# The weights' low parts written by ScalarE and an adding DMA instead of VectorE

## The chip, the cores and the metric

The kernel runs on one core of a Trainium2 chip. The metric is the device time of one execution in microseconds; the kernel before takes 945.7 us (median of three runs, 945.38 to 946.27).

## What is computed

One layer of a hybrid decoder trunk on 512 tokens of width 1024 in float32: a norm, three token mixers on one combined projection (windowed attention, a Conformer convolution of 31 taps, a gated short convolution), a gated merge, an output projection with residual, a gated MLP with a convolution of three taps, and a final norm. Cut to its core:

```python
u = rms_norm(x, norm1_g) @ w_in            # q k v | conf_a conf_gate | sc_b sc_c sc_x | gates
attn  = attention(q, k, v) @ w_attn_out
conf  = silu(layer_norm(dwconv31(conf_a * sigmoid(conf_gate)))) @ w_conf_out
short = (sc_b * dwconv3(sc_c * sc_x)) @ w_sc_out
x = x + (g0 * attn + g1 * conf + g2 * short) @ w_o
f_gate, f_val = split(dwconv3(rms_norm(x, norm2_g) @ w_up))
return rms_norm(x + (silu(f_gate) * f_val) @ w_down, final_g)
```

## The kernel before

**Weights.** All matrices are packed on the host in the order in which they are used: 1280 blocks of 128x128, eight to a chunk, so 160 chunks of 128x1024 float32 (512 KB each, `wts[c]`). TensorE takes each number as two parts, `hi` (the number cast to fp32r) and `lo` (the rest, cast too). A block is multiplied in three matmuls, hi·hi, hi·lo and lo·hi (`mm3`, L189 to L193; `down`, L845 to L847), so a chunk is 24 matmuls of 512 columns.

**The stream.** `prep(c)` (L150) loads chunk c from the SyncE queue into a float32 tile `w32` (L157; four buffers), and `w_split` makes the parts: ScalarE casts `w32` to `hi` (L170), VectorE subtracts, `lo = w32 - hi` (L171). `hi` and `lo` have `WB` = 4 buffers each. `take` (L177) hands out blocks and calls `prep` up to `AHEAD` = 2 chunks ahead of the one in use. A load thus waits until the subtraction has freed a `w32` buffer, and a cast until TensorE has done with the chunk that held the `hi` buffer. Chunks 0 and 1 are loaded in pieces at the start of the program, between the loads of x (L212 to L222), and split in quarters between the splits of x (L316).

**Who sets the order.** Each engine and each queue runs its instructions in a fixed order, in which a framework's scheduler has put them by readiness and by their place in the source; `tc.issue_after(q)` keeps what follows behind `q` on its engine. `anchor[0]` holds the last subtraction of a chunk's split, and the convolution's taps (a queue of VectorE tasks, `Queue.run`, L282) are put behind it. The zeros that `k_blocks` writes (L444) and the last norm's product (L874) are GpSimd's only other work.

**Other places that the rows name.** L237 and L238 split x for the first products (`xg`); L787, L790 and L812 evacuate and convolve a tile of the MLP's first product; L656 and L657 load two constants after the Conformer's products; the last three chunks (`KEEP` = 3, L890 to L896) are used a token tile at a time, then the final norm follows.

Of the kernel before, what the change touches and what calls it, by code (L numbers as in the profile page):

```python
# [10 lines left out]
F32 = mybir.dt.float32  # L11
# [28 lines left out]
GAP = 2  # L40
BUSY, FREE = 2.4, 2.7

# columns of the packed per-channel parameters
G1, G2 = 0, 8
CW = 16
CB = CW + KC * CONF_K
# [4 lines left out]
NPAR = FW + 2 * KF * 3  # L51


# the branches in the order of their merge: matrix, place of the gate, row blocks
BRANCHES = (("w_sc_out", 2, KC), ("w_attn_out", 0, 2), ("w_conf_out", 1, KC))


def weight_units():
    """The order in which 128x128 blocks of the weights are used: (matrix, row block, column block)."""
    aw = CONF // P  # L60
    a0, g0 = 18, 18 + aw
    b0, c0, x0 = 30, 36, 42
    gate0 = 48
    u = []
    for j in range(KC):
        for k in range(KD):
            u += [("w_in", k, a0 + j), ("w_in", k, g0 + j)]
    for g in range(3):
        for m in (0, 6):
            for p in range(2):  # L70
                u += [("w_in", k, m + 2 * g + p) for k in range(KD)]
        if g == 0:
            for k in range(KD):
                u += [("w_in", k, 12 + p) for p in range(2)]
    for k in range(KD):
        u += [("w_in", k, 14 + p) for p in range(4)]
    for j in range(KC):
        for m in (c0, x0, b0):
            u += [("w_in", k, m + j) for k in range(KD)]
    for name, br, n in BRANCHES:  # L80
        for s in range(KD + 1):
            if s < KD:
                u += [("w_in", k, gate0 + br * KD + s) for k in range(KD)]
            if s >= 1:
                u += [(name, k, s - 1) for k in range(n)]
    for j in range(KD):
        u += [("w_o", k, j) for k in range(KD)]
    for j in range(KF):
        for m in (j, KF + j):
            u += [("w_up", k, m) for k in range(KD)]  # L90
    for k in range(KF):
        u += [("w_down", k, c) for c in range(KD)]
    assert len(u) == N_UNITS
    return u


def score_bias():
    """ALiBi and the masks, by head pair: [4, 128, 512], from shapes alone."""
    slopes = np.exp2(-8.0 * np.arange(1, N_HEADS_ALL + 1, dtype=np.float32) / np.float32(N_HEADS_ALL)).astype(np.float32)
    i = np.arange(P)  # L100
    out = np.zeros((4, P, 512), np.float32)
    q, k = i[:, None], np.arange(256)[None, :]
    steps = q + P - k
    ok = (steps >= 0) & (steps <= 128)
    for p in range(2):
        for h in range(2):
            b = np.where(ok, -(slopes[2 * p + h] * steps.astype(np.float32)), np.float32(NEG))
            out[p, :, h * 256 : (h + 1) * 256] = b
    s1 = i[:, None] - i[None, :]
    s2 = s1 // 4  # L110
    ok1 = (s1 >= 0) & (s1 <= 128)
    ok2 = (s1 >= 0) & (s2 <= 128) & (s1 % 4 == 0)
    for p in range(2):
        for h in range(2):
            b1 = np.where(ok1, -(slopes[4 + 2 * p + h] * (s1 * 4).astype(np.float32)), np.float32(NEG))
            b2 = np.where(ok2, -(slopes[8 + 2 * p + h] * (s2 * 16).astype(np.float32)), np.float32(NEG))
            out[2 + p, :, h * 256 : h * 256 + 128] = b1
            out[2 + p, :, h * 256 + 128 : (h + 1) * 256] = b2
    return out
# [10 lines left out]
def trunk(ctx: ExitStack, tc: tile.TileContext, xT, wts, par, bias, sel, ident, fg, out):  # L130
# [13 lines left out]
    def ps512(name="ps"):  # L144
        return pp.tile([P, 512], F32, tag="ps", name=name)

    # ---- the stream of weights: loaded, and split into two parts that TensorE takes exactly
    chunks = {}

    def prep(c, load=((0, UNIT * P),), work=True):  # L150
        if c not in chunks:
            w32s[c] = wp.tile([P, UNIT * P], F32, tag="w32", name=f"w32_{c}", bufs=4)
            hi = wp.tile([P, UNIT * P], F32R, tag="whi", name=f"whi_{c}", bufs=WB)
            lo = wp.tile([P, UNIT * P], F32R, tag="wlo", name=f"wlo_{c}", bufs=WB)
            chunks[c] = (hi, lo)
        for a, b in load:
            nc.sync.dma_start(w32s[c][:, a:b], wts[c][:, a:b])  # L157
        if work:
            with ExitStack() as order:
                if c == 2:  # L160
                    for q in last:
                        order.enter_context(tc.issue_after(q))
                w_split(c, slice(0, UNIT * P))

    w32s = {}
    anchor = [None]

    def w_split(c, s):
        hi, lo = (q[:, s] for q in chunks[c])
        A.copy(hi, w32s[c][:, s])  # L170
        anchor[0] = V.tensor_tensor(out=lo, in0=w32s[c][:, s], in1=hi.bitcast(F32), op=ALU.subtract).ins  # L171

    WB = 4
    AHEAD = 2
    state = {"unit": 0, "prepped": 0}

    def take(n=1):  # L177
        """The next n blocks, as (hi, lo) of [128, n * 128]."""
        u = state["unit"]
        c, o = divmod(u, UNIT)  # L180
        assert o + n <= UNIT
        while state["prepped"] <= min(c + AHEAD, N_UNITS // UNIT - 1):
            prep(state["prepped"])
            state["prepped"] += 1
        state["unit"] += n
        hi, lo = chunks[c]
        return hi[:, o * P : (o + n) * P], lo[:, o * P : (o + n) * P]

    def mm3(ps, w, x, first, last):  # L189
        """ps += w.T @ x, each given as its two parts."""  # L190
        T.matmul(ps, w[0], x[0], start=first, stop=False)  # L191
        T.matmul(ps, w[0], x[1], start=False, stop=False)  # L192
        T.matmul(ps, w[1], x[0], start=False, stop=last)  # L193

    # ---- inputs and constants
    zero = cp.tile([P, WIDE], F32R, name="zero")
    V.memset(zero.bitcast(F32), 0.0)
    warm = ps512("warm")
# [29 lines left out]
    last = []  # L228

    def split(src, name, hi_scale=None, into=None):  # L230
        """Two parts of an SBUF or PSUM tile (times a per-partition factor)."""
        hi, lo = into or (t512(F32R, name + "h"), t512(F32R, name + "l"))
        if hi_scale is None:
            A.copy(hi, src)
# [15 lines left out]
        return split(acc, name + "s")  # L250

    def colsum(hi, lo, name):
        """Sums over all channels, on every partition: PSUM [128, 512]."""
        ps = ps512(name + "ps")
        T.matmul(ps, ones, hi, start=True, stop=False)
        T.matmul(ps, ones, lo, start=False, stop=True)
        return ps

    def rsqrt_of(ps, n, name):
        """(ps / n + eps) ** -0.5, with one Newton step."""  # L260
        a = t512(name=name + "a")
        V.tensor_scalar(out=a, in0=ps, scalar1=1.0 / n, scalar2=EPS, op0=ALU.mult, op1=ALU.add)
        y = t512(name=name + "y")
# [5 lines left out]
        V.scalar_tensor_tensor(out=r, in0=y, scalar=1.5, in1=r, op0=ALU.add, op1=ALU.mult)  # L269
        return r  # L270

    # ---- work that runs beside the matrix products, a little at a time
    class Queue:
        def __init__(self):
            self.q = deque()
# [14 lines left out]
        def drain(self):  # L290
            self.run(1e9)

    # ---- chains of work with TensorE in them: each link some slots after the one before it
    due = {}
    now = [0]
    starts = deque()
# [2 lines left out]
        due.setdefault(now[0] + n, []).append(fn)  # L299

    def slot():
        """Between two tiles of matrix products."""
        now[0] += 1
        for fn in due.pop(now[0], ()):
            fn()
        if starts and now[0] % EVERY == 0:
            starts.popleft()()
        conv.run(BUSY if due else FREE)

    # ---- first norm: the products start on x * g, and the rows' factors come in behind them  # L310
    xg = []
    for k in range(KD):
        with ExitStack() as order:
# [22 lines left out]

    hn = [None] * KD

    # ---- Conformer branch: gated input, 31 taps, layer norm, SiLU
    conv = Queue()  # L340
    apad = []
    cacc = [None] * KC
# [73 lines left out]

        conv.add(mean_sum, 5)

    # ---- attention
    def perm(ap):  # L420
        """Tokens by their residue modulo 4."""
        return ap.rearrange("p (i c) -> p c i", c=4)

    def qk_tile(name, permuted):
# [11 lines left out]
        return hi, lo  # L436

    def k_blocks(name):
        """The keys of two heads, by token tiles: the first head's rows beside the second's, zeros elsewhere."""
        hi, lo = (kp.tile([P, 1024], F32R, tag="kb", name=name + n) for n in "hl")  # L440
        v = lambda q, h: q[h * HD : (h + 1) * HD].rearrange("p (t h i) -> p t h i", t=4, h=2)
        for q in (hi, lo):
# [13 lines left out]
    stats = {}  # L456

    def v_tiles(s, n):
        """Values with the tokens on partitions: n columns for each of the four token tiles."""
        pss = [ps512(f"pv{s}{t}") for t in range(4)]  # L460
        for k in range(KD):
            wh, wl = take(n // P)
# [17 lines left out]
        slot()  # L480

    def block(s, t, p, qk, nm, l):
        """Two heads' scores, weights and weighted values for one tile of queries."""
        n = 128 if (s == 0 and t == 0) else 256
        sc = t512(name=f"sc{s}{t}{p}")
        scv = sc[:, : 2 * n].rearrange("p (h k) -> p h k", h=2)
# [115 lines left out]
            tt(U[0, p], U[0, p], U[1, p], ALU.add)  # L602
            oT[p] = split(U[0, p], f"oT{p}")

    # ---- gated short convolution
    short = [None] * KC

    def sc_in(j):
# [20 lines left out]
                tt(y, ps, y, ALU.mult)  # L629
                short[j] = split(y, f"sh{j}")  # L630

    # ================= the layer, in order
    got = {}
    def factors():
        box["r1"] = rsqrt_of(colsum(*parts, "n1"), D, "n1")
# [45 lines left out]
    for j in range(KC):  # L681
        sc_in(j)

    # ---- the gated merge, a branch at a time
    mixed = [None] * KD

    def gate(j, br):
# [30 lines left out]
            before = g  # L718
    assert not due

    # ---- output projection, residual, second norm
    xr = []
    for k in range(KD):
        t = t512(name=f"xr{k}")
# [43 lines left out]
        A.copy(o, ps)  # L768
        x1t[t][hf] = o

    # ---- gated MLP
    ff = [None] * KF

    def up_mm(j, m, x):
# [48 lines left out]
    for h in range(2):  # L823
        nc.sync.dma_start(fg_sb[h], fg[:, h * 512 : (h + 1) * 512].broadcast_to([P, 512]))

    # ---- down projection: all tokens at once, and the last blocks a token tile at a time
    base = state["unit"] // UNIT

    def wd(k):
# [17 lines left out]
            T.matmul(o, fh, wl, start=False, stop=k == KF - 1)  # L847

    def rows_of(t, sums):
        """The rows' factors (sum / D + eps) ** -0.5, with one Newton step."""  # L850
        a = sp.tile([P, 1], F32, tag="fa", name=f"fa{t}")
        r = sp.tile([P, 1], F32, tag="fr", name=f"fr{t}")
        z = sp.tile([P, 1], F32, tag="fz", name=f"fz{t}")
# [7 lines left out]
        return r  # L861

    def residual(t, h):
        """The sum with the residual, and its squares' sum."""
        q = x1t[t][h]
        tt(q, acc[t, h], q, ALU.add)
        ss = sp.tile([P, 1], F32, tag=f"ss{h}", name=f"ss{t}{h}")
# [82 lines left out]
```

## Time and profile before

| | |
|---|---|
| time, median of three runs | 945.7 us (945.38 to 946.27) |
| span of the profiled execution | 944.0 us |
| TensorE busy | 932.7 us (99%) |
| VectorE busy | 624.1 us (66%), of it 196.4 us the subtractions L171 |
| ScalarE busy | 382.6 us (41%), of it 168.8 us the casts L170 |
| GpSimd busy | 14.1 us (1%) |
| DMA | 92.70 MB, 98 GB/s over the span |
| granted TensorE clock | 0.998 of full speed |

The profiled execution's own time is its span, 944.0 us; the median of the runs is 1.7 us above it, which lies outside the span. The page gives each engine's busy time, and the costliest groups of instructions with the idle time of their engine before them and what ended it; further views of the same execution give windows of time, instructions in order of time, and what waited for what.

### The profile page before, as it was taken

Reading aid. Unit: us, or ns where it says so; the run is one execution under the profiler, and the core shown is the slowest. Engines: PE = TensorE matmul, PEld = TensorE weight load, DVE = VectorE, ACT = ScalarE, POOL = GpSimd, SP = SyncE. Lnnn points to the kernel's source line nnn. Section 1 sums busy time; section 2 is a strip of 40 time slices with the busy share of each in tenths; the row PEclk is TensorE's granted clock in tenths of the full one; section 3 lists DMA queues with packets and bytes.
Section 4 is the critical chain, followed back from the end, with each engine's and each line's share of the span. In section 5 each row is a group of like instructions: output and inputs, shape, how many; then the busy total and the mean of one; then the engine's idle time right before and its main releaser. Section 6 shows DMA issues by size and latency. Waiting matters only on the chain.

```text
span 944.0 us, 10726 instructions
## 1 busy us (share of the span) xinstructions
PE 932.7 (99%) x4214; PEld 764.2 (81%) x4214; DVE 624.1 (66%) x843; ACT 382.6 (41%) x581; POOL 14.1 (1%) x24
## 2 busy tenths in 40 slices
PE   8999999999999999999999999999999999999996
PEld 6888878988887888888888888888888888888885
DVE  6889887889789986585444557895555555632225
ACT  7442355345544322465333344564333333521114
POOL 3000000000000000000000000000000000000002
PEclk9999999999999999999999999999999999999999
DMA  8324322222122332223223522232222232323302
GB/s 278 111 90 156 100 80 70 87 85 72 67 67 68 111 112 90 90 97 103 90 90 103 187 89 90 94 107 91 90 89 90 91 109 90 108 94 104 97 0 90
DMA packets 28138, 92.70 MB, mean 98 GB/s; under 512 B 3252, under 2 KB 3640, under 8 KB 28088
## 3 DMA queue, kind: packets, MB, share of 16 engines
q1 hardware_dynamic: 28088, 92.02, 29.0%
q8 instruction: 33, 0.54, 0.2%
q14 instruction: 17, 0.14, 0.0%
HBM read 89.91 MB, written 2.10 MB: 97 GB/s over the span
## 4 chain that ended last, share of the span: by engine, by line
PE 97%; DVE 1%; DMA 1%; ACT 0%; SPq 0%; issue 0%; ACTq 0%
PE up L191 9%; PE up L193 9%; PE up L192 9%; PE gt L192 5%; PE gt L193 5%; PE gt L191 5%; PE dn L845 4%; PE dn L846 4%; PE dn L847 4%; PE mo L192 3%; PE mo L191 3%; PE mo L193 3%; PE wo L191 2%; PE wo L193 2%; PE wo L192 2%; PE pv L469 1%
## 5 line engine op out<-in xcount | busy, mean ns | idle before, releaser
L171 DVE TENSOR_TENSOR wlo<-w,whi 128x1024 fp32r<-128x1024 f32 (+1 forms) x166 | 196.4, 1183 | 230.6 <-ACT whi L170 229.9
L170 ACT CAST whi<-w 128x1024 fp32r<-128x1024 f32 (+1 forms) x166 | 168.8, 1017 | 362.4 <-issue 89.3
L372 DVE SCALAR_TENSOR_TENSOR cc<-ca,par_sb,cc 128x512 f32<-128x512 f32 x180 | 125.5, 743 | 0.2
L790 DVE SCALAR_TENSOR_TENSOR uc<-up,par_sb,uc 128x511 f32<-128x511 f32 (+1 forms) x76 | 56.1, 745 | 1.2
L243 DVE TENSOR_TENSOR sg<-mo,sg 128x512 f32<-128x512 f32 x24 | 16.5, 689 | 21.1 <-PE mo L193 19.6
L512 ACT ACTIVATE sc<-sc,nm 128x256 f32<-128x256 f32 (+1 forms) x32 | 15.6, 490 | 35.4 <-DVE nm L510 35.4
L812 ACT ACTIVATE uc<-uc 128x512 f32<-128x512 f32 x22 | 13.9, 632 | 37.9 <-DVE uc L790 37.8
L787 ACT ACTIVATE uc<-up,par_sb 128x512 f32<-128x512 f32 x38 | 25.8, 683 | 0.0
L845 PE MATMUL dn<-whi,fb 128*128 128x512 f32 x64 | 25.2, 394 | 0.0
L846 PE MATMUL dn<-whi,fb 128*128 128x512 f32 x64 | 25.2, 394 | 0.0
L847 PE MATMUL dn<-wlo,fb 128*128 128x512 f32 x64 | 25.2, 394 | 0.0
L692 ACT ACTIVATE sg<-gt 128x512 f32<-128x512 f32 x24 | 14.2, 597 | 23.7 <-PE gt L193 23.6
L874 POOL TENSOR_TENSOR x1t<-x1t,fg 128x512 f32<-128x512 f32 x4 | 5.6, 1389 | 922.4 <-ACT jk L869 922.4
L243 DVE TENSOR_TENSOR xr<-wo,xr 128x512 f32<-128x512 f32 x8 | 5.5, 692 | 17.9 <-PE wo L193 17.9
L243 DVE TENSOR_TENSOR ff<-uc,uc 128x512 f32<-128x512 f32 x22 | 15.2, 692 | 1.0 <-ACT uc L812 0.2
L191 PE MATMUL up<-h20h,whi 128*128 128x512 f32 x38 | 15.6, 410 | 0.0
L191 PE MATMUL up<-h24h,whi 128*128 128x512 f32 x38 | 15.1, 397 | 0.0
L191 PE MATMUL up<-h23h,whi 128*128 128x512 f32 x38 | 15.1, 397 | 0.0
L192 PE MATMUL up<-h25l,whi 128*128 128x512 f32 x38 | 15.1, 397 | 0.0
L191 PE MATMUL up<-h27h,whi 128*128 128x512 f32 x38 | 15.1, 397 | 0.0
L193 PE MATMUL up<-h27h,wlo 128*128 128x512 f32 x38 | 15.1, 396 | 0.0
L191 PE MATMUL up<-h22h,whi 128*128 128x512 f32 x38 | 15.0, 396 | 0.0
(1198 smaller groups left out, 2620.1 us busy)
## 6 DMA issues: line engine op xcount, KB each, us to landing
w<-wts SPq DMA_DIRECT2D x158, 512.0 KB, 3.2
xT<-xT SPq DMA_DIRECT2D x8, 256.0 KB, 5.4
xr<-xT SPq DMA_DIRECT2D x8, 256.0 KB, 5.2
out<-x1t SPq DMA_DIRECT2D x8, 256.0 KB, 2.1
bias<-bias SPq DMA_DIRECT2D x4, 256.0 KB, 4.8
w<-wts SPq DMA_DIRECT2D x2, 256.0 KB, 5.6
fg<-fg SPq DMA_DIRECT2D x2, 256.0 KB, 4.3
w<-wts SPq DMA_DIRECT2D x1, 384.0 KB, 4.0
```

What stands on the lines that cost most here:

```text
L170: A.copy(hi, w32s[c][:, s])
L171: anchor[0] = V.tensor_tensor(out=lo, in0=w32s[c][:, s], in1=hi.bitcast(F32), op=ALU.subtract).ins
L191: T.matmul(ps, w[0], x[0], start=first, stop=False)
L192: T.matmul(ps, w[0], x[1], start=False, stop=False)
L193: T.matmul(ps, w[1], x[0], start=False, stop=last)
L243: V.tensor_tensor(out=out, in0=a, in1=b, op=op)
L372: return lambda: V.scalar_tensor_tensor(out=cacc[j], in0=apad[j][:, t : t + 512], scalar=pc(CW + j * CONF_K + t), in1=cacc[j], op0=ALU.mul ...
L787: A.activation(c, ps, AF.Copy, scale=pc(w + 2))
L790: V.scalar_tensor_tensor(out=c[:, d:], in0=ps[:, : 512 - d], scalar=pc(w + t), in1=c[:, d:], op0=ALU.mult, op1=ALU.add)
L845: T.matmul(o, fh, wh, start=k == 0, stop=False)
L846: T.matmul(o, fl, wh, start=False, stop=False)
L847: T.matmul(o, fh, wl, start=False, stop=k == KF - 1)
```

## The change

From chunk 2 on `prep` makes both parts without VectorE and without SyncE: a DMA from GpSimd's queue casts the chunk as it loads it, straight into `hi`; ScalarE writes `-hi` into `lo`; a second DMA from GpSimd's queue reads the same chunk from memory again and adds it to `lo`. `w32` keeps two buffers, for chunks 0 and 1; `WB` goes to 5 and `AHEAD` to 3. `anchor[0]` is no longer set after chunk 1.

```diff
     def prep(c, load=((0, UNIT * P),), work=True):
         if c not in chunks:
-            w32s[c] = wp.tile([P, UNIT * P], F32, tag="w32", name=f"w32_{c}", bufs=4)
+            if c < 2:
+                w32s[c] = wp.tile([P, UNIT * P], F32, tag="w32", name=f"w32_{c}", bufs=2)
...
+        if c >= 2:
+            hi, lo = chunks[c]
+            nc.gpsimd.dma_start(hi, wts[c])
+            with ExitStack() as order:
+                if c == 2:
+                    for q in last:
+                        order.enter_context(tc.issue_after(q))
+                anchor[1] = A.activation(lo, hi.bitcast(F32), AF.Copy, scale=-1.0).ins
+            nc.gpsimd.dma_start(lo, wts[c], accum_op=ALU.add)
+            return
         for a, b in load:
             nc.sync.dma_start(w32s[c][:, a:b], wts[c][:, a:b])
...
-    anchor = [None]
+    anchor = [None, None]
...
-    WB = 4
-    AHEAD = 2
+    WB = 5
+    AHEAD = 3
```

## Rows read from the trace of the kernel before

**Rows 1.** The page: busy time by engine; the granted clock in 40 slices.

```profile
PE 932.7 (99%) x4214; PEld 764.2 (81%) x4214; DVE 624.1 (66%) x843; ACT 382.6 (41%) x581; POOL 14.1 (1%) x24
...
PEclk9999999999999999999999999999999999999999
```

**Rows 2.** Busy time by window: engines' busy us (instructions), clock, DMA share, GB/s.

```profile
core 0: us, PE busy (x) PEld busy (x) DVE busy (x) ACT busy (x) POOL busy (x), PEclk, DMA share, GB/s
...
20.00:114.00 94.00, 94.00 (x459) 78.49 (x459) 82.60 (x118) 36.71 (x50) 0.00 (x0) 1.00 0.35 118
...
180.00:297.00 117.00, 117.00 (x579) 98.28 (x579) 101.10 (x141) 54.74 (x104) 0.00 (x0) 1.00 0.23 77
...
565.00:815.00 250.00, 250.00 (x1099) 202.96 (x1098) 156.00 (x190) 105.93 (x144) 0.00 (x0) 1.00 0.28 93
815.00:930.00 115.00, 115.00 (x496) 92.80 (x495) 38.44 (x48) 30.41 (x41) 2.58 (x2) 1.00 0.23 77
930.00:944.00 14.00, 5.82 (x26) 4.37 (x24) 7.87 (x25) 5.46 (x16) 2.97 (x2) 0.87 0.33 123
```

**Rows 3.** Waits of TensorE: what waited for what, total us, times, longest.

```profile
PE warm L200 <- DVE zero L197: 1.2, 1, 1.2
PE pa L191 <- ACT xg1h L237: 1.1, 1, 1.1
PE pa L192 <- DVE xg0l L238: 0.3, 1, 0.3
```

**Rows 4.** The page's groups: out<-in, count, busy, mean ns, idle before, releaser.

```profile
L171 DVE TENSOR_TENSOR wlo<-w,whi 128x1024 fp32r<-128x1024 f32 (+1 forms) x166 | 196.4, 1183 | 230.6 <-ACT whi L170 229.9
L170 ACT CAST whi<-w 128x1024 fp32r<-128x1024 f32 (+1 forms) x166 | 168.8, 1017 | 362.4 <-issue 89.3
L372 DVE SCALAR_TENSOR_TENSOR cc<-ca,par_sb,cc 128x512 f32<-128x512 f32 x180 | 125.5, 743 | 0.2
```

**Rows 5.** Weight loads of TensorE in the MLP: start us, us, engine, line.

```profile
701.41 0.19 PEld L191 LDWEIGHTS up<-h20h,whi 128*128 128x128 f32 x1
...
706.97 0.19 PEld L191 LDWEIGHTS up<-h20h,whi 128*128 128x128 f32 x1
```

**Rows 6.** ScalarE and VectorE there, in order of time; idle before in brackets.

```profile
701.60 1.05 ACT L170 CAST whi<-w 128x1024 fp32r<-128x1024 f32 x1 [1.08 <-PE up L192]
702.56 0.68 ACT L787 ACTIVATE uc<-up,par_sb 128x512 f32<-128x512 f32 x1
...
702.68 1.23 DVE L171 TENSOR_TENSOR wlo<-w,whi 128x1024 fp32r<-128x1024 f32 x1 [2.89 <-ACT whi L170]
```

**Rows 7.** DMA: issues with KB and us to landing; one queue's bytes; issue times.

```profile
w<-wts SPq DMA_DIRECT2D x158, 512.0 KB, 3.2
...
q1 hardware_dynamic: 28088, 92.02, 29.0%
...
L157 SPq DMA_DIRECT2D w<-wts x162: 327/328/737, 0.7 to 893.3; - x162
```

**Rows 8.** GpSimd's instructions by line: count, busy us, mean ns.

```profile
L874 POOL TENSOR_TENSOR x1t<-x1t,fg 128x512 f32<-128x512 f32 x4 | 5.6, 1389 | 922.4 <-ACT jk L869 922.4
```

**Rows 9.** Start of the program in order of time: GpSimd, the SyncE queue, ScalarE, TensorE.

```profile
0.74 1.07 POOL L444 MEMSET kb10h<- 64x512 f32 x2 [0.29 <-POOLq L943]
...
8.47 0.50 PE L191 MATMUL pa<-xg1h,whi 128*128 128x512 f32 x1 [1.13 <-ACT xg1h L237]
...
8.99 1.91 SPq L157 DMA_DIRECT2D w<-wts  x3
11.01 0.36 SPq L656 DMA_DIRECT2D ident_sb<-ident  x1
...
14.56 14.27 SPq L157 DMA_DIRECT2D w<-wts  x6
...
14.85 1.05 ACT L170 CAST whi<-w 128x1024 fp32r<-128x1024 f32 x1 [0.84 <-DMA w<-wts]
```

**Rows 10.** The first windows, columns as in group 2.

```profile
5.00:10.00 5.00, 3.15 (x10) 1.89 (x11) 2.72 (x5) 2.80 (x7) 4.36 (x9) 1.00 0.99 320
10.00:15.00 5.00, 5.00 (x23) 3.99 (x23) 5.00 (x11) 4.16 (x10) 0.00 (x0) 1.00 1.05 406
```

**Rows 11.** TensorE's last matmul.

```profile
935.43 0.40 PE L847 MATMUL dn<-wlo,fh21h 128*128 128x512 f32 x1
```

## The prediction

> **What bounds the kernel now.** I read the page's busy times first: TensorE is busy for 932.7 of the 944.0 us, VectorE for 624.1, ScalarE for 382.6, GpSimd for 14.1, and the clock stays at its full level, 2.4 GHz [rows 1]. Next the windows: in those shown from 20 to 930 us TensorE's busy time equals the window, with VectorE at 83 to 101 us of windows of 94 and 117 us; only the start and the last 14 us have idle time [rows 2]. Then TensorE's waits: the longest are 1.2 and 1.1 us, all before 9 us [rows 3]. So TensorE's own work is the bound. VectorE is well used and late for nothing; its subtractions (196.4 us in all) lie beside matmuls [rows 4]. What TensorE asks of the stream is read from the MLP: the same block position begins at 701.41 and 706.97, so a chunk lasts 5.56 us, or 0.232 us a matmul [rows 5]. The cast for three chunks on starts the moment the last reader of its buffer is done (released by TensorE, L192) [rows 6]: the stream runs as far ahead as its buffers let it.
>
> **What is removed.** 158 subtractions of 1.23 us on VectorE [rows 6], about 190 us. Nothing on the path waits for them, so the gain in the middle is zero; what would be late next is TensorE itself. At most the idle time of the start and the tail could shrink. The SyncE queue loses 158 issues of 0.33 us [rows 7], also beside other work; its loads of constants and x get earlier, for nothing. VectorE's taps (180 of 0.743 us [rows 4]) lose the pacing by `anchor[0]`, which stays at chunk 1's last subtraction: a tap may then stand ahead of an evacuation and delay it by 0.74 us. No matmul waits for VectorE there, and eight PSUM tiles cover it: zero; without the cover 180 x 0.743 = 134 us at the very most, which I don't put in the range, since VectorE has the subtractions' time to spare.
>
> **What is added.** ScalarE: one pass of the same shape takes the cast's place, 1.05 us [rows 6]: no change in busy time. It reads SBUF as before. But it now waits for a load that the same loop has just ordered, and behind it on ScalarE stand the tile's evacuations (L787 among them), for which VectorE and in the end the PSUM tiles wait.
> DMA: 158 x 0.524 = 83 MB more. The old 92.02 MB took 29.0% of 16 engines' span, 274 us [rows 7], so 512 KB take 1.56 us. In sum 29% + 26% of the old span, or 29% + 52% if the add costs its time twice: there is room, by share.
> GpSimd: 316 issues, its own order, and waits. Here is the price.
>
> **The serial loop.** The order on GpSimd's queue is the scheduler's, by readiness: the rows show that it moves work that is ready ahead of work that isn't (the constant of L656 is issued at 11.01 us, after five chunks' loads, though twelve stand before it in the source; the zeros of L444 run at 0.74 us) [rows 9]. So when is what ready? Call the load into `hi` H and the add A, and g the time of an issue on GpSimd. No row has such an issue: SyncE's takes 0.33 us [rows 7], GpSimd's longest instruction 1.39 us [rows 8]. I take 0.8, between them. H from issue to landing is 3.2 us from SyncE [rows 7], so 3.2 - 0.33 + 0.8 = 3.67. A hand-over costs 0.03 us (cast end 702.65, subtraction 702.68 [rows 6]). From a free buffer to a ready add: 3.67 + 0.03 + 1.05 + 0.03 = 4.78 us, while the next buffer comes free 5.56 us later. So A(c) is ready before H(c+1), and the queue becomes H, A, H, A. GpSimd waits in A(c) for ScalarE, and H(c+1) stands behind it. In that order no two chunks overlap: one period is A's issue, H's issue and landing, and the negation. If A's transfer takes a, H's packets come behind it in the same queue and wait a - g more. So the period is T = 4.78 + g + (a - g) = 4.78 + a.
> The add reads the chunk and the old `lo`, and writes once. Bounds: a = 1.56, as a plain load, and 3.12, both reads in full. I take 2.0, nearer to the plain load, whose row it resembles in the HBM read and the write. T = 6.78 us against 5.56. The bounds: g = 0.33 with a = 1.56 gives 3.2 + 1.11 + 1.56 = 5.87; g = 1.39 with a = 3.12 gives 8.5. An add that stays clear of H altogether gives 4.78 + 0.8 = 5.58, the loop's floor at my g.
> A third reading, that the add's compute slows it further, has no row; it would only lie above.
> On the price of an add, the Trainium skill (Collectives: The Full Stack, "The bandwidth ceiling: the fold count and why AG ≠ RS ≠ AR") says that a reduce step of the DMA engines runs at half a copy's rate, since both sources are read by one ring, and not because of the arithmetic. By it T would be 7.9 us and the time 1271 us. No run here shows it yet.
>
> **The sum.** Chunk 2's cast ends at 15.9 us [rows 9]; H of chunks 2 to 4 needs no buffer, so the first three adds are 1.05 us apart and A(4) is issued at 18.0. From there 155 periods to A(159): 18.0 + 155 x 6.78 = 1069. Landing 3.2. Then TensorE has 72 matmuls of the last three chunks (16.7 us), 6 of which (1.4) didn't need the last one: 15.3. From its last matmul's end, 935.8, to the end of the span 8.2 us [rows 11]. Span 1069 + 3.2 + 15.3 + 8.2 = 1096, and 1.7 for what lies between span and median: 1097 us. In general 46.4 + 155 T: the loop sets the time when T is above 5.80. The 12 us by which the five buffers let the stream lead (22.2 less some 10 for H, negation, A) are used up after ten chunks.
>
> **The start.** `hi` of chunks 2 to 4 is free at once, and GpSimd has nothing that stands before those loads, as its zeros at 0.74 us show [rows 9]. 1.57 MB thus meet the loads of x and chunk 0 in 5 to 15 us, where the DMA engines are at 99 to 105% at 320 to 406 GB/s [rows 10]; before, the SyncE queue issued them at 9 to 10.9 us [rows 9]. In full that is 1.57 MB / 0.36 = 4.3 us, and TensorE is waiting for x there (its matmul on xg1 at 8.47 us [rows 9]). Between 0 and 4.3 us; I take 3. In the forecast it lies inside the rounding of T.
>
> **The rivals.**
> *The stream keeps up* (not slower). The same loop with T at or below 5.80, or a queue order that lets it overlap: where ScalarE is busy when H lands, or H lands later than I have it, A(c) becomes ready over 0.78 us later than my 4.78, so H(c+1) is put ahead of A(c). Then two chunks are in flight and a pair needs 4.78 + a or some 7 us, half of what TensorE needs for two (11.1). For it: ScalarE has instructions of 0.6 to 0.7 us at just these places, and one such pair in three is enough. Against it: ScalarE is idle for 1.08 us and more before the casts [rows 6] and at 41% at all. Then the time is 945.7 plus the start: within 947.6 if GpSimd's first loads come late or share well, else 947.6 to 951, say 949.
> *The add costs twice or more*: the same loop with T from 7.6 to 8.5, 1225 to 1364 us. For it: two operands to read. Against: the second one is in SBUF.
> *VectorE's relief shows*: a shorter start (no subtraction in front of the norm's sums) or tail, 1 to 4 us, 942 to 944. For it: VectorE and ScalarE alternate in the last 8.2 us. Against: no subtraction lies in that tail and TensorE's early waits are for x's parts, not for weights [rows 3].
> That the change does not do what it says, a load that casts nothing and an add of zeros, costs the same transfers and gives the same times.
>
> **How the numbers follow.** About 0.2%, 1.9 us, is what a measurement of this kernel tells from no change. Forecast (paced by the loop, T from 5.87 to 7.6, 956 to 1225 us): 0.46. Double add, 1225 to 1364: 0.12. Keeps up with a dearer start, 947.6 to 956: 0.22. Keeps up, within 0.2%: 0.15. Faster: 0.05. So faster 0.05, same 0.15, slower 0.80. The predicted time is the forecast's, 1097 us. The range goes from 945 us, which leaves out the faster cases and the lower part of the same ones (0.08), to 1280 us, which leaves out the dearest adds (0.08).
>
> **What would show it.** Right: on GpSimd's queue loads and adds strictly in turn; the negations (`lo` written from `hi`) spaced by T, each released by a DMA; TensorE waiting for `wlo` in each chunk, its busy time unchanged at some 933 us; VectorE down by 190 us. The steps apart: g is GpSimd's issue, a the add's landing less a load's. Wrong: two loads in a row on GpSimd's queue and no wait of TensorE after 20 us mean that the stream keeps up; then only the first 20 us differ. A negation released by ScalarE's own earlier work would mean that the loop goes through ScalarE's order instead. If TensorE's clock falls in the gaps, to 1.2 GHz, matmuls lengthen from 0.39 us and the time lies above the sum.

## The result

The changed kernel takes 1109.3 us (median of three runs, 1109.2 to 1113.7) against 945.7: a ratio of 1.174, with a 95% interval of 1.171 to 1.177. The forecast was 1097 us, range 945 to 1280. The mechanism behind it, a loop through GpSimd's queue, is the one that the runs show; but two of its numbers were wrong and cancelled, as told below.

The page of the kernel after, its parts 1 to 3 and 5, answers to [rows 1, 4, 7]. TensorE's busy time has grown from 932.7 to 991.6 us and its idle time from 11.3 to 120.3; the clock has gaps; the queue q0 is GpSimd's.

```profile
span 1111.9 us, 10849 instructions
...
PE 991.6 (89%) x4214; PEld 790.2 (71%) x4214; DVE 442.8 (40%) x685; ACT 374.7 (34%) x581; POOL 241.0 (22%) x340
...
PEclk9998999999998999899998898999999999899998
...
q0 software_dynamic: 45504, 165.70, 64.5%
...
L164 ACT ACTIVATE wlo<-whi 128x1024 fp32r<-128x1024 f32 x158 | 167.1, 1058 | 631.8 <-DMA whi<-wts 605.8
L165 POOL DMA_DIRECT2D wlo<-wts x158 | 138.7, 878 | 835.6 <-ACT wlo L164 793.4
L159 POOL DMA_DIRECT2D whi<-wts x158 | 124.7, 862 | 9.4 <-PE pg L204 5.3
...
whi<-wts POOLq DMA_DIRECT2D x158, 512.0 KB, 6.6
wlo<-wts POOLq DMA_DIRECT2D x158, 512.0 KB, 5.5
```

The loop stands in the idle times of part 5: ScalarE's negation (L164) waits for the load in 605.8 us, GpSimd's add (L165) waits for the negation in 793.4 us, and the load (L159) waits for almost nothing but its place in the queue, 9.4 us. If the buffers were the limit, that last number would be the large one. VectorE's busy time is down by 181 us, and it bought nothing.

Next come TensorE's longest waits in the kernel after; in the kernel before they were 1.2 us and less [rows 3]. Now 62 of its 120 us of idle time are waits for low parts, in five kinds of products, and most of the rest are waits for ScalarE and VectorE.

```profile
PE up L204 <- DMA wlo<-wts: 24.5, 14, 3.4
PE dn L858 <- DMA wlo<-wts: 19.5, 8, 5.7
PE wo L202 <- ACT mx7h L245: 7.9, 1, 7.9
PE gt L204 <- DMA wlo<-wts: 7.6, 5, 3.2
```

Those other waits can come from the stream too. In front of the single wait of 7.9 us, for `mx7h`, ScalarE sits idle for 7.80 us before a negation, and the cast of `mx7h` stands right behind it:

```profile
619.17 1.06 ACT L164 ACTIVATE wlo<-whi 128x1024 fp32r<-128x1024 f32 x1 [7.80 <-DMA whi<-wts]
620.13 0.60 ACT L245 CAST mx7h<-sg 128x512 fp32r<-128x512 f32 x1
```

GpSimd's queue and ScalarE in the MLP, in order of time. Adds (L165) and loads (L159) are not strictly in turn: after the add at 708.05 two loads follow (x2), after the one at 720.09 a single one.

```profile
708.05 0.89 POOL L165 DMA_DIRECT2D wlo<-wts  x1 [2.63 <-ACT wlo L164]
708.60 1.45 POOL L159 DMA_DIRECT2D whi<-wts  x2
716.24 0.89 POOL L165 DMA_DIRECT2D wlo<-wts  x1 [6.19 <-ACT wlo L164]
720.09 0.89 POOL L165 DMA_DIRECT2D wlo<-wts  x1 [2.97 <-ACT wlo L164]
720.64 0.91 POOL L159 DMA_DIRECT2D whi<-wts  x1
728.14 0.87 POOL L165 DMA_DIRECT2D wlo<-wts  x1 [6.60 <-ACT wlo L164]
...
714.88 1.06 ACT L164 ACTIVATE wlo<-whi 128x1024 fp32r<-128x1024 f32 x1 [0.99 <-DMA whi<-wts]
...
718.21 0.63 ACT L823 ACTIVATE uc<-uc 128x512 f32<-128x512 f32 x1 [1.05 <-DVE uc L801]
718.75 1.04 ACT L164 ACTIVATE wlo<-whi 128x1024 fp32r<-128x1024 f32 x1
```

A single turn, from the add at 720.09 to the one at 728.14, is 8.05 us; a pair, 708.05 to 720.09, is 12.04 us for two chunks. TensorE wants 5.56 a chunk. These are read from one place: in the mean of all, a turn with one load takes 8.8 us and one with two 10.6. Over the whole program the order that was compiled has 113 such turns for the 158 chunks: 70 with one load, 42 with two, and the first with four. From A(4) at 20.9 us to the last add at 1080.6 the mean period is 1059.7 / 155 = 6.84 us.

### The profile page after: what moved, and what is told of

Read it like the earlier page. It is cut to its first block, busy times and chain, and to the rows that moved or that the text cites. A ratio compares the mean times of both kernels' runs of the same rounds, so it can differ in the third digit from the quotient of the medians.

```text
span 1111.9 us, 10849 instructions
## 1 busy us (share of the span) xinstructions
PE 991.6 (89%) x4214; PEld 790.2 (71%) x4214; DVE 442.8 (40%) x685; ACT 374.7 (34%) x581; POOL 241.0 (22%) x340
## 3 DMA queue, kind: packets, MB, share of 16 engines
q0 software_dynamic: 45504, 165.70, 64.5%
## 4 chain that ended last, share of the span: by engine, by line
issue 63%; POOL 15%; PE 13%; DMA 6%; ACT 1%; DVE 1%; SPq 0%; POOLq 0%; ACTq 0%
POOL whi L159 9%; POOL wlo L165 7%; DMA wlo<-wts 3%; DMA whi<-wts 2%; PE gt L204 2%; PE gt L203 2%; PE gt L202 2%; PE dn L858 1%; PE mo L202 1%; PE dn L857 1%; PE mo L203 1%; PE dn L856 1%; PE mo L204 1%; DMA w<-wts 0%; PE up L204 0%
## 5 line engine op out<-in xcount | busy, mean ns | idle before, releaser
L164 ACT ACTIVATE wlo<-whi 128x1024 fp32r<-128x1024 f32 x158 | 167.1, 1058 | 631.8 <-DMA whi<-wts 605.8
L165 POOL DMA_DIRECT2D wlo<-wts x158 | 138.7, 878 | 835.6 <-ACT wlo L164 793.4
L159 POOL DMA_DIRECT2D whi<-wts x158 | 124.7, 862 | 9.4 <-PE pg L204 5.3
L254 DVE TENSOR_TENSOR x1t<-dn,x1t 128x512 f32<-128x512 f32 x8 | 5.5, 686 | 105.6 <-PE dn L858 105.6
L204 PE MATMUL up<-h20h,wlo 128*128 128x512 f32 x38 | 16.7, 438 | 24.5 <-DMA wlo<-wts 24.5
L204 PEld LDWEIGHTS up<-h20h,wlo 128*128 128x128 f32 x38 | 7.1, 187 | 31.7 <-DMA wlo<-wts 30.6
L823 ACT ACTIVATE uc<-uc 128x512 f32<-128x512 f32 x22 | 13.9, 631 | 34.0 <-DVE uc L801 34.0
L254 DVE TENSOR_TENSOR ptl<-pt,pth 128x512 fp32r<-128x512 f32 (+1 forms) x16 | 10.4, 651 | 35.2 <-ACT pth L534 35.2
L858 PEld LDWEIGHTS dn<-wlo,fb 128*128 128x128 f32 x64 | 12.7, 198 | 10.2 <-DMA wlo<-wts 7.1
L204 PE MATMUL up<-h22h,wlo 128*128 128x512 f32 x38 | 16.0, 421 | 0.0
L203 PE MATMUL up<-h22l,whi 128*128 128x512 f32 x38 | 16.0, 421 | 0.0
```

The costliest lines, as they stand in the source:

```text
L159: nc.gpsimd.dma_start(hi, wts[c])
L164: anchor[1] = A.activation(lo, hi.bitcast(F32), AF.Copy, scale=-1.0).ins
L165: nc.gpsimd.dma_start(lo, wts[c], accum_op=ALU.add)
L254: V.tensor_tensor(out=out, in0=a, in1=b, op=op)
```

## The experiments

Two theories were left by the result. **Loop:** the order on GpSimd's queue makes load, negation and add of one chunk wait for those of the chunk before. **Work:** the DMA engines (64.5% busy), or GpSimd's issues, are simply slower than they look. They differ in what happens when only the order changes.

**e1_turns: strictly in turn.** Each load is put behind the add before it.

```diff
-            nc.gpsimd.dma_start(hi, wts[c])
+            with ExitStack() as turn:
+                if adds:
+                    turn.enter_context(tc.issue_after(adds[-1]))
+                nc.gpsimd.dma_start(hi, wts[c])
...
-            nc.gpsimd.dma_start(lo, wts[c], accum_op=ALU.add)
+            adds.append(nc.gpsimd.dma_start(lo, wts[c], accum_op=ALU.add).ins)
```

> Each load into hi is put behind the add of the chunk before it on GpSimd's queue: strictly load, add, load, add. The changed kernel has some 2 loops for 3 chunks, and one add to the next over a single load took 8.05 us there (720.09 to 728.14). Loop theory: one loop for each chunk, 46.4 + 155 x 8.05 = 1294 us. Rival, the DMA engines' or GpSimd's total work sets the pace: the same work in another order, 1109 us.

1347.4 us, ratio 1.424 (1.421 to 1.427). The same work in another order costs 238 us more, so the work alone doesn't set the time. Its period, from the add of chunk 4 at 34.4 us to the last one at 1323.8, is 1289.4 / 155 = 8.32 us; the 8.05 read from one place was too short, and so was the expected 1294 us. GpSimd's queue (add, load, add, load) with one negation, and two lines of the page:

```profile
702.77 0.90 POOL L162 DMA_DIRECT2D whi<-wts  x1
709.56 1.06 ACT L167 ACTIVATE wlo<-whi 128x1024 fp32r<-128x1024 f32 x1 [3.79 <-DMA whi<-wts]
710.92 0.87 POOL L168 DMA_DIRECT2D wlo<-wts  x1 [7.25 <-ACT wlo L167]
711.46 0.88 POOL L162 DMA_DIRECT2D whi<-wts  x1
718.85 0.87 POOL L168 DMA_DIRECT2D wlo<-wts  x1 [6.51 <-ACT wlo L167]
...
q0 software_dynamic: 45504, 165.70, 53.8%
...
whi<-wts POOLq DMA_DIRECT2D x158, 512.0 KB, 6.2
```

**e2_ahead1: one load ahead of each add.** Same transfers and passes; the add of chunk c is put behind the load of c + 1.

```diff
-            nc.gpsimd.dma_start(hi, wts[c])
+            h = nc.gpsimd.dma_start(hi, wts[c]).ins
...
-            nc.gpsimd.dma_start(lo, wts[c], accum_op=ALU.add)
+            with tc.issue_after(h):
+                for k in range(max(2, c - 1), c + 1 if c == N_UNITS // UNIT - 1 else c - 0):
+                    nc.gpsimd.dma_start(chunks[k][1], wts[k], accum_op=ALU.add)
```

> The add of chunk c is put behind the load of chunk c+1, so that two chunks are always in flight; same transfers, same passes. Loop theory: a loop of 8 to 9 us now carries two chunks, 4.0 to 4.5 us each, under TensorE's 5.56: the stream keeps up and the time is 946 to 960 us. Rival, total work of the DMA engines: 1109 us. Rival, ScalarE's order holds the negations back: between the two, 1000 to 1109 us.

951.8 us, ratio 1.0055 (1.0038 to 1.0071): 158 of the 164 us are gone, by order alone. This carries the verdict. GpSimd's queue, its longest waits, and q0:

```profile
702.88 0.55 POOL L159 DMA_DIRECT2D whi<-wts  x1 [4.53 <-PE up L206]
703.42 0.91 POOL L167 DMA_DIRECT2D wlo<-wts  x1
708.43 0.55 POOL L159 DMA_DIRECT2D whi<-wts  x1 [4.10 <-PE up L206]
709.96 0.86 POOL L167 DMA_DIRECT2D wlo<-wts  x1 [0.98 <-ACT wlo L164]
...
POOL whi L159 <- PE up L206: 161.8, 43, 4.6
POOL wlo L167 <- ACT wlo L164: 71.3, 80, 4.2
...
q0 software_dynamic: 45504, 165.70, 81.2%
```

The roles are turned round: now the loads wait for TensorE (buffers), and the adds' wait for ScalarE has fallen from 793.4 to 71.3 us. TensorE sets the pace again, while the DMA engines are busier (81%) than in the slow kernel (64%).

**e4_plain_second: the second DMA doesn't add.** The same order as in the changed kernel; a second casting load overwrites the negative.

```diff
-            nc.gpsimd.dma_start(lo, wts[c], accum_op=ALU.add)
+            nc.gpsimd.dma_start(lo, wts[c])
```

> The second DMA doesn't add: it is a second casting load over the negative, with the same wait on ScalarE, so the low part is wrong. It prices the addition. If the add takes its transfer time twice, as a read of two operands, each loop loses some 1.5 us; 2 loops in 3 chunks, 155 x 1.0 less: 955 to 1000 us. If an add costs what a casting load costs: 1109 us as before.

951.1 us, ratio 1.0052 (1.0032 to 1.0073), just below the expected 955 to 1000. The bytes over the queue are the same, and so is the order of instructions on GpSimd and on ScalarE, and the time is 158 us less. So in the compiled order the loop is too long only with the price of an add; in strict turns it is too long without it too (e10_turns_plain, below). The page's q0 and issues:

```profile
q0 software_dynamic: 45504, 165.70, 54.3%
...
whi<-wts POOLq DMA_DIRECT2D x158, 512.0 KB, 4.4
wlo<-wts POOLq DMA_DIRECT2D x158, 512.0 KB, 3.6
```

**e5_no_add: no second DMA.** The adding line is left out, and with it the low part's addition.

```diff
-            nc.gpsimd.dma_start(lo, wts[c], accum_op=ALU.add)
```

> The adding DMA is left out: the low part is minus the high part. GpSimd's queue holds loads alone and waits for ScalarE no more. Loop theory and total work both say that the stream keeps up, 944 to 950 us. If it stays above 1000 us the cause is the casting load itself or ScalarE's wait for it, not the loop through GpSimd.

945.9 us, ratio 0.9999 (0.9989 to 1.0009). Loads by GpSimd and ScalarE's wait for them cost nothing; VectorE's 179 us less are worth nothing. From its page come the prices of a casting load:

```profile
q0 software_dynamic: 22752, 82.85, 28.0%
...
L159 POOL DMA_DIRECT2D whi<-wts x158 | 83.6, 529 | 815.8 <-PE up L203 191.0
...
whi<-wts POOLq DMA_DIRECT2D x158, 512.0 KB, 3.5
```

28.0% of 943.9 us over 158 loads is 1.67 us of the 16 engines for one. With it the add's price follows: in the kernel after (717 us of q0 - 158 x 1.67) / 158 = 2.87 us, in e1_turns 2.91, and in e2_ahead1, where loads and adds run side by side, 3.2.

**e10_turns_plain: strictly in turn, without adding.** e1_turns with e4's edit, to test the sum of one loop.

```diff
-            adds.append(nc.gpsimd.dma_start(lo, wts[c], accum_op=ALU.add).ins)
+            adds.append(nc.gpsimd.dma_start(lo, wts[c]).ins)
```

> Strict turns as in e1_turns, but the second DMA is a plain second casting load (low part wrong). It tests the sum of one loop: landing alone 3.5 us, negation 1.06, hand-overs 0.1, and the transfer ahead in the queue, now 1.63 us where the add takes 2.9. T = 4.66 + 1.63 = 6.3 us, 46.4 + 155 x 6.3 = 1023 us. If the loop has a part that the sum lacks, as e1_turns' 8.39 us against 4.66 + 2.9 = 7.5 suggest, 0.86 us more each: 1156 us. If the add's own processing and not its transfer is what paces, the loop is short: 950 us.

1081.8 us, ratio 1.144 (1.138 to 1.149), between the 1023 and the 1156 us of the expectation. GpSimd, ScalarE and TensorE run the same sequence of instructions as in e1_turns, so the addition alone is worth 266 us here, 1.7 us a chunk. By the trace T is 6.60 us, 0.31 above the sum's 6.29, where e1_turns' 8.32 lies 0.76 above its 7.56. So the sum is right in kind and a part is missing. Some 0.3 us of it is in both runs, between the end of the negation (L167) and the issue on GpSimd that waits for it: 0.33 us in the mean here and 0.34 in e1_turns, where the sum had 0.1 for all hand-overs. It is seen in both runs' lines, here from 712.90 to 713.20:

```profile
707.09 0.54 POOL L162 DMA_DIRECT2D whi<-wts  x1
...
711.32 0.63 ACT L827 ACTIVATE uc<-uc 128x512 f32<-128x512 f32 x1 [1.66 <-DVE uc L805]
711.86 1.04 ACT L167 ACTIVATE wlo<-whi 128x1024 fp32r<-128x1024 f32 x1
...
713.20 0.53 POOL L168 DMA_DIRECT2D wlo<-wts  x1 [5.57 <-ACT wlo L167]
```

ScalarE's own work stands in the loop too, at some places: this load landed at 711.41, but the negation starts at 711.86, behind the SiLU of a tile. It is little in the mean: from a load's landing to its negation pass 0.17 us here and 0.11 in e1_turns, of which 0.08 (the median) passes where nothing stands in the way. What e1_turns lacks beyond that, some 0.4 us, lies in the landing of a load behind an add, 6.27 us in the mean.

**e8_high_by_scalar: the load by SyncE.** `hi` is cast by ScalarE from a SyncE load as before the change, then negated; only the adds are GpSimd's.

```diff
-            if c < 2:
+            if True:
                 w32s[c] = wp.tile(...)
...
-            nc.gpsimd.dma_start(hi, wts[c])
+            nc.sync.dma_start(w32s[c], wts[c])
...
+                A.copy(hi, w32s[c])
                 anchor[1] = A.activation(lo, hi.bitcast(F32), AF.Copy, scale=-1.0).ins
```

> The load leaves GpSimd's queue: SyncE loads the chunk as before the change, ScalarE casts it to hi and then writes the negative (two passes, 2.1 us a chunk), GpSimd's queue holds the adds alone. Loop theory: no load stands behind an add any more, so the stream keeps up although DMA moves as many bytes and ScalarE does more: 945 to 952 us. If the add's wait for ScalarE or its transfer were the cause: 1050 us and more.

951.4 us, ratio 1.0057 (1.0037 to 1.0077), although ScalarE's busy time is 536 us instead of 375. A second way to take the load out from behind the add, with the same effect.

**e9_start_old and e11_sel_later: what is left of e2_ahead1.** Both have its edit and look for its last 6 us. In e9 chunks 2 and 3 are also made the old way, with four buffers of `w32`, `hi` and `lo`.

```diff
-            if c < 2:
+            if c < 4:
...
-                w32s[c] = wp.tile([P, UNIT * P], F32, tag="w32", name=f"w32_{c}", bufs=2)
+                w32s[c] = wp.tile([P, UNIT * P], F32, tag="w32", name=f"w32_{c}", bufs=4)
...
-        if c >= 2:
+        if c >= 4:
...
-    WB = 5
+    WB = 4
```

> As e2_ahead1 (one load ahead of each add), but chunks 2 and 3 are still loaded by SyncE and split by ScalarE and VectorE, with four buffers of w32, hi and lo. It asks what the 5.6 us are that e2_ahead1 keeps. If they are the start (chunk 2's add lands 3.1 us late, and the clock falls in 20 to 30 us): 945.5 to 947 us. If they are the stream itself (the DMA engines at 81 to 98%, PSUM or buffers): still 950 to 952 us. If VectorE's relief is worth anything it shows here: below 945 us.

948.8 us (five runs, 948.5 to 952.0), ratio 1.0046 (1.0030 to 1.0062). Between the two answers: the start is clean, TensorE is busy throughout 10 to 30 us as before, and up to 909 us of the profiled execution it is 0.4 to 1.2 us ahead of the kernel before, so neither the stream nor the DMA engines hold it back on the way. But it now waits at the end for low parts; I put that down to the four buffers, which wasn't tried by itself:

```profile
PE dn L860 <- DMA wlo<-wts: 3.7, 2, 2.5
```

In e11 the start is left to the new way, and a constant's cast that ScalarE's order had moved into the start is put back.

```diff
-    A.copy(sel_sb, sel32)
+    with tc.issue_after(anchor[1]):
+        A.copy(sel_sb, sel32)
```

> As e2_ahead1 (one load ahead of each add), and the cast of the small constant sel_sb is put behind a later negation on ScalarE. In the changed kernel and in e2_ahead1 it stands in front of the split of xg5 and waits 2.5 us for its DMA; in the kernel before it runs at 23.1 us, after the start. If the 3.1 us that TensorE waits for chunk 2's low part come from that wait, the add of chunk 2 is issued at 15.5 instead of 18.0 us and lands at 20.9, where TensorE wants it at 20.4: 946 to 948 us, without the fall of the clock. If the add would be late at the start anyway: 950 to 952 us. Below 945 us only if VectorE's relief is worth something.

948.8 us, ratio 1.0023 (1.0014 to 1.0033), 3 us better than e2_ahead1 and just above the expected 948. TensorE still waits 2.8 us for chunk 2's low part:

```profile
16.33 0.90 POOL L167 DMA_DIRECT2D wlo<-wts  x1 [2.81 <-ACT wlo L164]
...
PE pa L206 <- DMA wlo<-wts: 2.8, 1, 2.8
```

The expected wait of 0.5 was too low at both ends. The add is issued at 16.33 us instead of 18.00 but not at the expected 15.5, because the negation starts right behind its load's landing at 14.95 us, 5.3 us after the issue. And TensorE, no longer held up before, wants the low part at 19.0 us and not at 20.4. The add's own landing, 5.4 us, was as expected. No version is faster than the kernel before.

## Why the prediction was right, and where only by luck

**TensorE is the bound and VectorE's relief is worth nothing: right.** e5_no_add, which has the relief without the adds, is at 0.9999 of the kernel before. The rival of the shorter start or tail has fallen.

**The serial loop: right.** e2_ahead1 and e1_turns edit nothing but the order on GpSimd's queue and lie 158 us below and 238 us above the change. The compiled order of the other engines moves a little with it in e2_ahead1 (27 of ScalarE's 581 instructions) and more in e1_turns (396); in e4_plain_second ScalarE's order and GpSimd's are the change's own, and only the second transfer's price is another.

**The queue becomes H, A, H, A: wrong.** This step put a ready add 4.78 us after a free buffer, 0.78 us ahead of the next load. The compiled order has 42 turns of two loads among 113. The sum then counted 155 loops, where the program has 113.

**T = 6.78 us for one loop: too low.** In strict turns it is 8.32 (e1_turns). Its terms, put in the prediction and measured in the mean of 155 loops: from an add's issue to the next load's, 0.8 and 0.54; from the load's issue to its landing behind the add, 4.87 (3.67 and a - g) and 6.27; the hand-over to the negation, 0.03 and 0.11; the negation, 1.05 and 1.06; from its end to the next add's issue, 0.03 and 0.34. So the step that failed is the load's landing behind an add. H alone was put at 3.67 and is 3.5 (e5_no_add); the mis-sized term is the add's transfer a, put at 2.0, which is 2.87 to 2.91. With it the sum gives 4.66 + 2.9 = 7.6. Of the rest to 8.32, some 0.3 us is the hand-over from ScalarE to GpSimd, and some 0.4 is more delay behind the add than a says. Behind an add a load's issue keeps GpSimd for 0.89 us and not for 0.53, which may be the reason; that wasn't tried.

**The two errors cancel.** 113 turns, 42 of them longer ones with two loads, make the same 6.84 us a chunk as 155 strict turns of my 6.78 would. With the right a and the strict order the forecast would have been 46.4 + 155 x 7.6, about 1220; with the true order and my own prices, 70 turns of 6.78 us and 42 pairs of 7, it would have been 5.0 us a chunk, a stream that keeps up. The forecast of 1097 us against 1109 is thus closer than its working deserves.

**"One such pair in three is enough": wrong.** The rival of the stream that keeps up took a pair for some 7 us. In the changed kernel more than a third of the turns are pairs, but a pair takes 10.6 us in the mean (9.3 to 14.2), and a single turn 8.8. The first load of a pair lands 6.3 us after its issue, behind the add, and the second 1.4 us later; from there to the second negation pass 0.9 us more in the mean. At the place shown it waits longer: the second load has landed at 716.05, but a SiLU (L823) that waits for VectorE stands ahead, and the negation starts at 718.75. So ScalarE's order, which the prediction named as a sign that it would be wrong, is a part of the loop in the pairs, though not the largest. A load ahead of every add was enough, as e2_ahead1 shows.

**The price of an add: nearly double.** It is the rival in which the add costs twice that had this right, with T from 7.6 to 8.5 us. The add takes 2.87 us of the engines against 1.67 for a casting load, 1.7 times, and 3.2 us, 1.9 times, where both run together. The Trainium skill (Collectives: The Full Stack, "The bandwidth ceiling: the fold count and why AG ≠ RS ≠ AR") has the reduce step of a collective at half a copy's rate, for its two reads. The trace of this adding DMA is nearer to that rule than to my 2.0. Whether the second read or the addition itself costs this was not tried.

**The start: the mechanism was wrong, the size of the wait about right.** I had nothing of GpSimd's standing before its first loads; its zeros stood there, and the loads went out at 9.64 us. The cost came another way: chunk 2's add is issued at 17.96 us, and TensorE waits for it at 23.45. In front of it, on ScalarE, the cast of `sel_sb` waits 2.5 us for its DMA. The kernel after, ScalarE's wait, GpSimd's first add and TensorE [rows 9]:

```profile
ACT sel_sb L669 <- DMA sel<-sel: 2.5, 1, 2.5
...
17.96 0.90 POOL L165 DMA_DIRECT2D wlo<-wts  x1 [4.02 <-ACT wlo L164]
...
23.45 0.50 PE L204 MATMUL pa<-xg0h,wlo 128*128 128x512 f32 x1 [3.06 <-DMA wlo<-wts]
```

The wait of 3.1 us lies in the 0 to 4.3 that I had given. In the slow kernel it hides in the loop. In e2_ahead1's profiled execution the start is the 6 us that are left: TensorE is 7 us late at 25 us and no later after that, by 3.1 us of waiting, nearly 3 of clock and the rest before 16 us. That can't be so in every run, for another run of e2_ahead1 took 951.8 us at a granted clock of 0.998.

**TensorE's busy time unchanged at 933 us: wrong.** It rose to 991.6 us: of the span's 168 us more, 109 are idle and 59 are busy. The granted clock fell to 0.952 in the mean, as the last line of the prediction had for a possibility, and 205 matmuls at half the clock, 0.62 us each against 0.39, make some 44 of the 59. The rest is at full clock: in e10_turns_plain busy time is 34 us up at a clock of 0.991. I take it for the overlap of neighbouring matmuls, which a wait breaks (one begins every 0.23 us and lasts 0.39); that wasn't tried. The clock was not the cause of the slow kernel: e10_turns_plain is paced by the stream with hardly any of it.

## What to carry to other kernels

When a load, an engine's pass and a second DMA of the same item are issued on one queue, look at the order of that queue: an issue that waits holds back the next item's load, and the engines' shares (here 64% of DMA, 22% of GpSimd) show nothing of it. Put the load of the next item ahead of the waiting issue by hand, as e2_ahead1 does; it was worth 158 us here. And work that is taken from an engine off the path, even 180 us of it as here, buys nothing.

## What the runs showed of the hardware

An issue of an adding DMA keeps GpSimd for 0.88 us. One of a casting load keeps it for 0.53 alone (e5_no_add), and for 0.89 right behind an adding one (e1_turns). An issue on GpSimd that waits for ScalarE starts 0.30 us after the pass has ended (median in e1_turns), where VectorE started 0.03 us after the cast [rows 6]. A casting load from GpSimd lands 3.5 us after its issue when nothing stands ahead of it, against 3.2 for a plain one from SyncE [rows 7]; behind a second casting load it takes 4.4 us, and behind an adding one 6.2 (medians of e10_turns_plain and e1_turns).

A gap of 3.1 us in TensorE's work at the same place had two outcomes. In e2_ahead1's profiled execution the granted clock went to half, 1.2 GHz, for some 6 us behind it; in that of the kernel after it stayed at 1.00 up to 32 us. The windows of the two, first e2_ahead1, columns as in [rows 2]:

```profile
22.00:24.00 2.00, 0.48 (x1) 0.49 (x2) 1.79 (x3) 2.00 (x5) 0.35 (x1) 0.69 1.06 199
24.00:26.00 2.00, 2.00 (x6) 1.52 (x6) 1.65 (x3) 0.70 (x1) 0.86 (x1) 0.50 1.06 209
26.00:28.00 2.00, 2.00 (x7) 1.51 (x6) 0.00 (x0) 0.00 (x0) 0.00 (x0) 0.50 1.02 213
```

then the kernel after:

```profile
22.00:24.00 2.00, 0.55 (x2) 0.48 (x3) 1.79 (x3) 2.00 (x5) 0.30 (x1) 1.00 1.08 205
24.00:26.00 2.00, 2.00 (x10) 1.65 (x9) 1.60 (x3) 0.66 (x1) 0.86 (x1) 1.00 1.03 199
```
